# Hybrid decoder block: value products stored unfolded, division on the loaded outputs, key duplicates by DMA, twelve early gate tiles

## The chip, the core and the metric
The kernel runs on one core of a Trainium2 chip. The metric is device time in microseconds (us), the median of the runs. The engines are TensorE (PE: matmuls and transposes, with its weight loads shown as PEld), VectorE (DVE), ScalarE (ACT), GpSimd (POOL) and SyncE (SP). Each runs its own instructions in a fixed order and waits on semaphores for the others; SP and ScalarE also issue the DMAs.

## What is computed
One layer of a decoder block on x of 1024 positions by 1024 features, in float32. Four causal mixers read the same normalised input; each output is projected, gated and summed.

```python
h = rms_norm(x, norm_attn_pre)
(a_q, a_kv, a_g, b_qkv, c_qkv, c_f, d_qlat, d_kvlat, d_krope) = split_cols(h @ w_in, IN_SPLITS)
o_a = nsa_mixer(...)         # 4 heads: compressed, selected and window branch, gated
o_b = dilated_mixer(...)     # 2 heads x 3 dilations, merged by their denominators
o_c = forgetting_mixer(...)  # 4 heads, log-forget bias on the logits
o_d = mla_mixer(...)         # 4 heads, low-rank keys and values
for i, (o_i, w_i) in enumerate(branches):     # A, B, C, D
    term = sigmoid(h @ w_merge_gate[i]) * (o_i @ w_i)
    merged = term if i == 0 else merged + term
x = x + rms_norm(merged @ w_o, norm_attn_post)
```

Each attention is a softmax over the causal keys, `p / den` times the values, with a head of 64 features. A gated MLP of width 2816 with a causal convolution follows; the change does not touch it.

## The kernel before
Every float32 operand of a large product is split into two parts, `hi` (rounded) and `lo` (the remainder), and `gemm` (lines 136 to 144) runs three matmuls for each 128 rows of depth: hi by hi (L142), hi by lo (L143), lo by hi (L144). A split costs one copy on ScalarE (L119 for weights, L316 and L336 for projections) and one subtraction on VectorE or GpSimd (L120, L320).

The attention stage (to about 735 us) first makes the normalised input `H`, then runs the mixers in the order D (141 to 262), A (262 to 476), C (476 to 604) and B (604 to 731). `project` writes 512 columns of a projection into the PSUM tile `pd`; `k_pair`, `q_pair` and `v_pair` make operands of it. `k_pair` keeps two heads, each twice, on both halves of the 128 partitions, since the hi and lo queries lie in opposite halves: four ScalarE copies of 64 partitions for each 512 columns, two or four remainders on VectorE, and in the unshared form one GpSimd copy for each head.

For one head, groups of 256 queries are worked off: `softmax_rows` makes the logits `ps` of a block of 128 queries, VectorE adds the bias and takes the maximum (L382), ScalarE the exponential with the row sum `den` (L387); `normalize` takes the reciprocal (L394) and multiplies the block (L396, or L398 with a gate). `pv` then transposes the probabilities (`ptp`, L419), splits them into `th` (ScalarE) and `tl` (VectorE), and multiplies by the values (L434 to L437) into `pvt`. The upper and lower 64 partitions of `pvt` hold the hi and the lo part of the values' product, so `fold` (L443, L444) copies one half on VectorE and adds the other, into the output tile `ot`. A pair of heads fills 128 partitions of `ot`, which ScalarE's queue stores to `o_d` in HBM.

The gates are products of `H` with 128 output features m, for a branch br. `FILL` names seven (br, m) that are computed early: `fill_tile` loads two weight chunks through a single buffer `fraw`, splits them into `fh` (ScalarE) and `fl` (GpSimd), runs two halves of 24 matmuls into the single PSUM buffer `pf` at a priority far below all else, and ScalarE applies tanh (`ft`, L206) and stores to `gate_d`. The program is ordered ahead of time by a scheduler that goes by priorities and its own estimates; on the chip each engine's order is fixed.

In the stage after that (`p2`, 740 to 1089) seven output tiles are loaded (`oraw`, two buffers, L930, by ScalarE's queue) and split into `oh` and `ol`. For m = 0 to 7 then come, in the branch order D, A, C, B (3, 0, 2, 1), the gate's product `pgb` (48 matmuls, none if it is early) and the branch's product (12, and 6 for B), and VectorE and GpSimd sum into `merged`. The out-projection and the MLP follow. [rows n] further on names a group of rows of the trace, which stand in their own section below.

Of the kernel before, what the change touches and what calls it, by code (L numbers as in the profile page):

```python
# [15 lines left out]
F32 = mybir.dt.float32  # L16
# [3 lines left out]
ALU = mybir.AluOpType  # L20
# [13 lines left out]
NFILL = 7  # L34
# [51 lines left out]
def body(tc, a, out):  # L86
# [10 lines left out]
    o_d = drp.tile([896, S], F32, name="o_d")  # L97
# [16 lines left out]
    miscc = cp.tile([128, 384], F32, name="miscc")  # L114
    ident, tri, ones = miscc[:, 0:128], miscc[:, 128:256], miscc[:, 256:384]
# [60 lines left out]
    with ExitStack() as c1:  # L176
# [152 lines left out]
        def k_pair(src, kind="n", shared=False):  # L329
            ks = [ap.tile([128, S], F32R, name="ks", tag="ks", bufs=BUFS["ks"]) for _ in range(2)]  # L330
            kl = [ap.tile([128, S], F32R, name="kl", tag="kl", bufs=BUFS["kl"]) for _ in range(2)]
            for hf, ps in project(src):
                for e in range(2):
                    pe = ps[64 * e:64 * e + 64]
                    for d in range(2):
                        A.copy(permuted(ks[e][64 * d:64 * d + 64], hf, kind), psin(pe, kind))  # L336
                    if shared:
                        for d in range(2):
                            lo_of(permuted(kl[e][64 * d:64 * d + 64], hf, kind),
                                  permuted(ks[e][64 * d:64 * d + 64], hf, kind), pe, kind)  # L340
                    else:
                        lo_of(permuted(kl[e][64 * e:64 * e + 64], hf, kind),
                              permuted(ks[e][64 * e:64 * e + 64], hf, kind), pe, kind)
            if not shared:
                for e in range(2):
                    o = 64 - 64 * e
                    G.tensor_copy(kl[e][o:o + 64], kl[e][64 * e:64 * e + 64].bitcast(F32))
            return ks, kl
# [18 lines left out]
        def softmax_rows(chunks, clamp=BIG, stat=None, two=False, into=None):  # L367
# [18 lines left out]
            den = nm[:, 6:7] if stat is None else stat[1]  # L386
# [3 lines left out]
        def normalize(P, n, den, nm, gate=None, guard=False):  # L390
# [4 lines left out]
            if gate is None:  # L395
                V.tensor_scalar(P[:, 0:n], P[:, 0:n], rc, None, op0=ALU.mult)  # L396
            else:
                V.tensor_scalar(P[:, 0:n], P[:, 0:n], rc, gate, op0=ALU.mult, op1=ALU.mult)  # L398
# [47 lines left out]
        def new_pv():  # L446
            return psv.tile([128, 256], F32, name="pvt", tag="pv")

# [127 lines left out]
        hx = ap.tile([128, 2, 64], F32, name="hx")  # L576
# [7 lines left out]
        u = ap.tile([128, 128], F32, name="u")  # L584
# [83 lines left out]
        for pr in range(2):  # L668
# [23 lines left out]
            fill()  # L692
            ot = new_ot()
            for e in range(2):
                (qh, ql), (kh, kl_) = QD[e], KD[e]
# [19 lines left out]
        ks, kl = k_pair(a["win"][1], shared=True)  # L715
        va = v_pair(a["win"][2])
        for pr in range(2):
            qs = q_pair(a["win"][3 + pr])
            ot = new_ot()
            for e in range(2):  # L720
                h = 2 * pr + e
                fill()
                bias = toeplitz(h)
                for g in range(4):
# [30 lines left out]
                    fold(ot[64 * e:64 * e + 64, 256 * g:256 * g + 256], pvt, e)  # L755
            A.dma_start(o_d[128 * pr:128 * pr + 128, :], ot)
# [3 lines left out]
        for pr in range(2):  # L760
# [3 lines left out]
            ot = new_ot()  # L764
            for e in range(2):
                h = 2 * pr + e
                fill()
                nck = ap.tile([128, S], F32, name="nck", tag="bias", bufs=BUFS["bias"])
# [5 lines left out]
                for g in range(4):  # L774
                    pvt = new_pv()
                    P2 = []
                    for qb in (2 * g, 2 * g + 1):
# [7 lines left out]
                        P, n, den, nm = softmax_rows(ch)  # L785
                        normalize(P, n, den, nm)
                        P2.append(P)
                    pv(pvt, P2, causal_blocks(vc[:, e], 2 * g + 2), True, True)
                    fold(ot[64 * e:64 * e + 64, 256 * g:256 * g + 256], pvt, e)
            A.dma_start(o_d[384 + 128 * pr:384 + 128 * pr + 128, :], ot)  # L790
# [94 lines left out]
        A.dma_start(o_d[256:384, :], ot0)  # L885
# [38 lines left out]
    with pool("p2") as p2:  # L924
        branches = ((3, 640, 2), (0, 0, 2), (2, 384, 2), (1, 256, 1))
        O = {}
        for br, f0, nk in branches:
            for k in range(nk):
                raw = p2.tile([128, S], F32, name="oraw", tag="oraw", bufs=2)
                A.dma_start(raw, o_d[f0 + 128 * k:f0 + 128 * k + 128, :])  # L930
# [4 lines left out]
        for m in range(KT):  # L935
# [5 lines left out]
            pgb = {}  # L941
            te = []
            for i in [i for i, f in enumerate(FILL) if f[1] == m]:
                for hf in range(2):
                    te.append(p2.tile([128, 512], F32, name="te", tag="te", bufs=2))
                    SP.dma_start(te[hf], gate_d[i][:, 512 * hf:512 * hf + 512])

            def gate(br):
# [3 lines left out]
                for hf in range(2):  # L952
                    pgb[br, hf] = pq("pgb", "qr"[hf])
                    if not early:
                        gemm(pgb[br, hf][:, 0:512], lambda k: (gh[:, k], gl[:, k]), h_half(hf), range(KT))

            def branch(br, f0, nk):
                early = (br, m) in FILL
                kt0 = f0 // 128
                for hf in range(2):  # L960
                    c = slice(512 * hf, 512 * hf + 512)
                    t = te[hf] if early else p2.tile([128, 512], F32, name="tg", tag="tg", bufs=2)
# [365 lines left out]
```

## Time and profile before

| | us |
|---|---|
| median of 3 runs | 1878.5 |
| lowest and highest | 1878.36, 1881.29 |
| the profiled execution, its own time | 1880.98 |
| its span in the trace | 1879.2 |
| mixers D to B (window) | 590 (141 to 731) |
| gate and branch stage (window) | about 350 (740 to 1089) |

The profile is one execution; its instructions are recorded with start and length, and idle time is put down to the engine whose signal ended it. The mean granted clock of TensorE over the span was 0.991 of full speed. A matmul's record overlaps the next one's, so busy time of PE is longer than the distance between matmuls.

### The profile page before, as it was taken

Reading aid. Unit: us, or ns where it says so; the run is one execution under the profiler, and the core shown is the slowest. Engines: PE = TensorE matmul, PEld = TensorE weight load, DVE = VectorE, ACT = ScalarE, POOL = GpSimd, SP = SyncE. Lnnn points to the kernel's source line nnn. Section 1 sums busy time; section 2 is a strip of 40 time slices with the busy share of each in tenths; the row PEclk is TensorE's granted clock in tenths of the full one; section 3 lists DMA queues with packets and bytes.
Section 4 is the critical chain, followed back from the end, with each engine's and each line's share of the span. In section 5 each row is a group of like instructions: output and inputs, shape, how many; then the busy total and the mean of one; then the engine's idle time right before and its main releaser. Section 6 shows DMA issues by size and latency. Waiting matters only on the chain.

```text
span 1879.2 us, 24134 instructions
## 1 busy us (share of the span) xinstructions
PE 1817.5 (97%) x8894; PEld 1489.8 (79%) x8894; DVE 1092.4 (58%) x2110; ACT 789.7 (42%) x1467; POOL 527.6 (28%) x520
## 2 busy tenths in 40 slices
PE   7889999999999899999999999899999999999998
PEld 6767777877777787888888878688888888888786
DVE  4438869989877344322222265688676767733544
ACT  5435646656565453312112144444443434332432
POOL 3401121221122210111222201597767675100000
PEclk9999999999999999999999999899999999999999
DMA  7151110100111112311222142122222222444643
GB/s 240 49 139 41 53 58 25 36 23 24 35 44 55 31 46 85 111 63 56 76 66 61 40 179 90 59 101 90 79 76 82 79 90 68 148 144 151 224 153 111
DMA packets 55366, 158.83 MB, mean 85 GB/s; under 512 B 9344, under 2 KB 10704, under 8 KB 55248
## 3 DMA queue, kind: packets, MB, share of 16 engines
q1 hardware_dynamic: 42352, 124.09, 20.6%
q10 hardware_dynamic: 12896, 33.21, 5.0%
q8 instruction: 70, 1.15, 0.3%
q14 instruction: 48, 0.39, 0.1%
HBM read 129.91 MB, written 31.61 MB: 86 GB/s over the span
## 4 chain that ended last, share of the span: by engine, by line
PE 68%; DVE 3%; DMA 1%; ACT 1%; issue 1%; POOL 0%; SPq 0%; DVEq 0%; ACTq 0%; POOLq 0%
PE pgb L142 6%; PE pgb L143 6%; PE pgb L144 6%; PE pk L1219 4%; PE pk L1221 4%; PE pk L1220 4%; PE py L143 2%; PE py L142 2%; PE pz L143 2%; PE pz L142 2%; PE py L144 2%; PE pz L144 2%; PE px L143 2%; PE px L142 2%; PE px L144 2%; PE pd L142 2%
## 5 line engine op out<-in xcount | busy, mean ns | idle before, releaser
L142 PE MATMUL pgb<-hh,whi 128*128 128x512 f32 x400 | 155.8, 390 | 1.1 <-ACT ft L206 0.7
L144 PE MATMUL pgb<-hh,wlo 128*128 128x512 f32 x400 | 155.6, 389 | 0.0
L143 PE MATMUL pgb<-hl,whi 128*128 128x512 f32 x400 | 155.6, 389 | 0.0
L120 DVE TENSOR_TENSOR wlo<-wraw,whi 128x1024 fp32r<-128x1024 f32 x25 | 30.6, 1225 | 210.4 <-ACT whi L119 210.4
L119 ACT CAST whi<-wraw 128x1024 fp32r<-128x1024 f32 x38 | 40.0, 1053 | 233.4 <-PE pgb L143 196.3
L387 ACT ACTIVATE P<-P,nm 128x512 f32<-128x512 f32 (+7 forms) x160 | 108.1, 677 | 64.6 <-DVE nm L382 63.4
L1086 POOL TENSOR_TENSOR aset<-sums,aset 128x512 fp32r<-128x512 f32 x66 | 131.2, 1988 | 5.3 <-ACT aset L1085 5.2
L142 PE MATMUL pd<-hh,whi 128*128 128x512 f32 x320 | 129.9, 406 | 2.1 <-DVE kl L320 2.0
L425 ACT CAST th<-ptp 128x512 fp32r<-128x512 f32 (+3 forms) x202 | 96.7, 517 | 77.8 <-PE ptp L419 65.5
L144 PE MATMUL pd<-hh,wlo 128*128 128x512 f32 x320 | 129.0, 403 | 0.0
L143 PE MATMUL pd<-hl,whi 128*128 128x512 f32 x320 | 129.0, 403 | 0.0
L426 DVE TENSOR_TENSOR tl<-ptp,th 128x512 fp32r<-128x512 f32 (+3 forms) x202 | 115.3, 599 | 17.5 <-ACT th L425 15.3
L1219 PE MATMUL pk<-aset 128*128 128x512 f32 x320 | 124.6, 390 | 0.6 <-DVE y L1259 0.6
L1220 PE MATMUL pk<-aset 128*128 128x512 f32 x320 | 124.5, 390 | 0.5 <-DVE aset L120 0.5
L1221 PE MATMUL pk<-aset 128*128 128x512 f32 x320 | 124.3, 390 | 0.0
L974 POOL TENSOR_TENSOR mg<-mg,tg 128x512 f32<-128x512 f32 x32 | 42.1, 1319 | 286.1 <-DVE tg L972 241.7
L419 PE MATMUL ptp<-miscc,P 128*128 128x128 f32 x678 | 112.2, 274 | 5.9 <-DVE P L396 3.1
L423 POOL MEMSET th<- 128x128 f32 x86 | 18.9, 220 | 291.2 <-PE pvt L434 130.7
L1085 ACT CAST aset<-wraw 128x512 fp32r<-128x512 f32 x88 | 54.1, 618 | 97.7 <-PE pz L144 37.8
L419 PEld LDWEIGHTS ptp<-miscc,P 128*128 128x128 f32 x678 | 80.4, 140 | 15.5 <-DVE P L396 4.9
L120 DVE TENSOR_TENSOR aset<-at,aset 128x512 fp32r<-128x512 f32 x44 | 30.4, 692 | 106.9 <-ACT aset L119 106.8
L1085 ACT CAST aset<-sums 128x512 fp32r<-128x512 f32 x66 | 40.9, 622 | 119.5 <-PE py L144 37.1
(362 smaller groups left out, 5109.5 us busy)
## 6 DMA issues: line engine op xcount, KB each, us to landing
wraw<-in_wup SPq DMA_DIRECT2D x44, 512.0 KB, 3.6
wraw<-in_wdn SPq DMA_DIRECT2D x44, 512.0 KB, 3.5
wraw<-in_wg SPq DMA_DIRECT2D x25, 512.0 KB, 3.5
act_d<-o ACTq DMA_DIRECT2D x22, 512.0 KB, 3.9
at<-act_d SPq DMA_DIRECT2D x44, 256.0 KB, 2.6
wraw<-in_win SPq DMA_DIRECT2D x20, 512.0 KB, 3.2
x<-in_x SPq DMA_DIRECT2D x8, 512.0 KB, 6.9
wraw<-in_wo SPq DMA_DIRECT2D x8, 512.0 KB, 3.5
```

What stands on the lines that cost most here:

```text
L142: T.matmul(ps, lh, rh, start=first and ii == 0, stop=False)
L143: T.matmul(ps, lh, rl, start=False, stop=False)
L144: T.matmul(ps, ll, rh, start=False, stop=last and ii == n - 1)
L387: A.activation(P[:, 0:c0], P[:, 0:c0], AF.Exp, bias=prev, scale=-1.0, accum_out=den)
L419: T.transpose(tp[0:kr, at[x]], P2[x[1]][:, c:c + kr], ident)
L425: A.copy(th[0:kr, i0:i1], tp[0:kr, i0:i1])
L426: V.tensor_tensor(tl[0:kr, i0:i1], tp[0:kr, i0:i1], th[0:kr, i0:i1].bitcast(F32), op=ALU.subtract)
L1085: A.copy(t[:, 0], src)
L1086: eng.tensor_tensor(t[:, 1], src, t[:, 0].bitcast(F32), op=ALU.subtract)
L1219: T.matmul(ps[b][:, w], ah[:, c], wh[:, w], start=st, stop=False)
L1220: T.matmul(ps[b][:, w], ah[:, c], wl[:, w], start=False, stop=False)
L1221: T.matmul(ps[b][:, w], al[:, c], wh[:, w], start=False, stop=sp)
```

## The change
- The output tiles of A, C and D hold one head each, unfolded: ScalarE copies the whole 128x256 `pvt` into `ot`, and `keep` stores the two halves of 64 partitions into two planes of `o_d`. B still folds.
- C and D do not normalise their probabilities. Their row sums go into `dens`, whose reciprocal is taken once after C.
- In `p2` each output of A, C and D is loaded as two tiles (both through `oraw`) and added on VectorE. For C and D, ScalarE spreads the reciprocals over a tile, PE transposes it in eight blocks (`rcp`), and VectorE multiplies.
- `k_pair` makes one copy and one remainder of all 128 partitions, and six DMAs on SP's queue make the duplicates.
- `NFILL` goes from 7 to 12: the tiles (1,0), (2,7), (2,6), (2,5) and (2,4) are early as well. D calls `fill` once for each head.
- Early gate tiles are loaded from `gate_d` where the gate would be computed, into `tg` with four buffers. `hx` and `u` share buffers with `th` and `tl`.

```diff
-NFILL = 7
+NFILL = 12
...
-    o_d = drp.tile([896, S], F32, name="o_d")
+    o_d = drp.tile([2, 896, S], F32, name="o_d")
...
+    dens = cp.tile([128, 8, 8], F32, name="dens")
...
             for hf, ps in project(src):
-                for e in range(2):
-                    pe = ps[64 * e:64 * e + 64]
-                    for d in range(2):
-                        A.copy(permuted(ks[e][64 * d:64 * d + 64], hf, kind), psin(pe, kind))
...
+                hi, lo = permuted(ks[0], hf, kind), permuted(kl[0], hf, kind)
+                A.copy(hi, psin(ps, kind))
+                lo_of(lo, hi, ps, kind)
+            for t in (ks, kl):
+                for d in range(2):
+                    SP.dma_start(t[1][64 * d:64 * d + 64].bitcast(F32), t[0][64:128].bitcast(F32))
+                SP.dma_start(t[0][64:128].bitcast(F32), t[0][0:64].bitcast(F32))
...
+        def keep(row, ot):
+            for d in range(2):
+                A.dma_start(o_d[d, row:row + 64, :], ot[64 * d:64 * d + 64])
...
-                        P, n, den, nm = softmax_rows(causal_chunks(mk, qb, 0, 128 * qb + 128, causal))
-                        normalize(P, n, den, nm)
-                        P2.append(P)
+                        P2.append(softmax_rows(causal_chunks(mk, qb, 0, 128 * qb + 128, causal),
+                                               den=dens[:, qb, 4 + 2 * pr + e:5 + 2 * pr + e])[0])
                     pv(pvt, P2, causal_blocks(vd[pr][:, e], 2 * g + 2), True, True)
-                    fold(ot[64 * e:64 * e + 64, 256 * g:256 * g + 256], pvt, e)
-            A.dma_start(o_d[640 + 128 * pr:640 + 128 * pr + 128, :], ot)
+                    A.copy(ot[:, 256 * g:256 * g + 256], pvt)
+                keep(640 + 128 * pr + 64 * e, ot)
...
+        V.reciprocal(dens, dens)
...
                 raw = p2.tile([128, S], F32, name="oraw", tag="oraw", bufs=2)
-                A.dma_start(raw, o_d[f0 + 128 * k:f0 + 128 * k + 128, :])
+                A.dma_start(raw, o_d[0, r, :])
+                if br != 1:
+                    raw2 = p2.tile([128, S], F32, name="oraw", tag="oraw", bufs=2)
+                    A.dma_start(raw2, o_d[1, r, :])
+                    V.tensor_tensor(raw, raw, raw2, op=ALU.add)
+                if br > 1:
+                    h = 4 * (br - 2) + 2 * k
+                    tp = pq("rcp", "qr"[k])
+                    A.copy(raw2.rearrange("p (b h d) -> p b h d", b=8, h=2),
+                           dens[:, :, h:h + 2].unsqueeze(3).to_broadcast([128, 8, 2, 64]))
+                    for b in range(8):
+                        T.transpose(tp[:, 128 * b:128 * b + 128], raw2[:, 128 * b:128 * b + 128], ident)
+                    V.tensor_tensor(raw, raw, tp, op=ALU.mult)
```

TensorE's order at the end of the gate tiles, where the first gate products follow: `pf` are matmuls of `fill_tile`, `pgb` those of the gates of `p2`, `hh` and `hl` the two parts of the input. Before:

```order
L142 MATMUL pf<-hh_116,fh 128x512
L143 MATMUL pf<-hl_117,fh 128x512
L144 MATMUL pf<-hh_116,fl 128x512
L142 MATMUL pgb<-hh_114,whi 128x512
L143 MATMUL pgb<-hl_115,whi 128x512
L144 MATMUL pgb<-hh_114,wlo 128x512
```

The same place after; `rcp` are the transposes of the spread reciprocals, eight for each output tile of C or D:

```order
L145 MATMUL pf<-hh_122,fh 128x512
L146 MATMUL pf<-hl_123,fh 128x512
L147 MATMUL pf<-hh_122,fl 128x512
L941 MATMUL rcp<-miscc,oraw 128x128 x24
L145 MATMUL pgb<-hh_120,whi 128x512
L146 MATMUL pgb<-hl_121,whi 128x512
L147 MATMUL pgb<-hh_120,wlo 128x512
```

The transposes of three output tiles now stand between the last gate tile and the first gate product; the fourth tile's stand 40 `pgb` matmuls further on. Of the `pf` matmuls 305 of 336 stood ahead of the last transposes of mixer B (`wtp`) before, and 239 of 576 now; the other 337 stand behind them in one piece.

ScalarE's order around the first loads of the outputs: `ft` are the tanh steps of the gate tiles and `gate_d` their stores, `oraw` the loads of outputs. Before:

```order
L206 ACTIVATE ft<-pf 128x512
L885 DMA o_d<-ot 128x1024
L207 DMA gate_d_99<-ft 128x512
L206 ACTIVATE ft<-pf 128x512
L207 DMA gate_d_99<-ft 128x512
L930 DMA oraw<-o_d 128x1024 x2
L119 CAST bh<-braw 128x896
L119 CAST oh_8118<-oraw 128x1024
L119 CAST oh_8124<-oraw 128x1024
L930 DMA oraw<-o_d 128x1024 x2
```

The same place after:

```order
L209 ACTIVATE ft<-pf 128x512
L210 DMA gate_d_104<-ft 128x512
L209 ACTIVATE ft<-pf 128x512
L210 DMA gate_d_104<-ft 128x512
L929 DMA oraw<-o_d 128x1024
L932 DMA oraw<-o_d 128x1024
L122 CAST bh<-braw 128x896
L938 COPY oraw<-dens 128x1024
L929 DMA oraw<-o_d 128x1024
L122 CAST oh_8253<-oraw 128x1024
L932 DMA oraw<-o_d 128x1024
```

The first load stands behind the last gate tile's store in both, but in the changed kernel that is the twelfth tile's, each output takes two loads, and the copy of the reciprocals and the split of one output stand between the loads of the next.

## Rows read from the trace of the kernel before
**Rows 1.** The page's first part: busy us, share of the span, instructions.
```profile
PE 1817.5 (97%) x8894; PEld 1489.8 (79%) x8894; DVE 1092.4 (58%) x2110; ACT 789.7 (42%) x1467; POOL 527.6 (28%) x520
```
**Rows 2.** Windows: us, busy PE, PEld, DVE, ACT, POOL; clock, DMA share, GB/s.
```profile
141.00:731.00 590.00, 570.39 (x3348) 463.47 (x3347) 452.99 (x1320) 336.22 (x749) 116.60 (x213) 1.00 0.12 39
846.00:940.00 94.00, 94.00 (x416) 77.83 (x416) 24.31 (x28) 18.71 (x24) 18.05 (x12) 1.00 0.20 66
```
**Rows 3.** Windows, instructions of pf alone (first) and of pgb alone (two).
```profile
733.30:739.00 5.70, 5.68 (x24) 4.42 (x24) 0.00 (x0) 1.00 0.35 138
...
739.86:793.70 53.84, 53.47 (x234) 43.95 (x235) 3.94 (x6) 3.78 (x7) 1.00 0.39 130
793.70:835.86 42.16, 42.16 (x187) 34.91 (x186) 5.27 (x8) 4.37 (x8) 1.00 0.19 51
```
**Rows 4.** Chain of waits in mixer B: start us, us, engine, tile, line.
```profile
686.32 0.95 PE ps L378 x8
...
690.49 0.87 PE ptp L419 x8
```
**Rows 5.** Groups of PE, 141 to 731: busy us, mean ns; idle before, releaser.
```profile
L142 PE MATMUL pd<-hh,whi 128*128 128x512 f32 x304 | 123.7, 407 | 2.1 <-DVE kl L320 2.0
...
L142 PE MATMUL pd<-wq,qnhi 128*128 128x384 f32 x2 | 0.7, 339 | 0.0
```
**Rows 6.** Groups of DVE, line L396: 141 to 262 (D), 476 to 604 (C).
```profile
L396 DVE TENSOR_SCALAR P<-P,nm 128x128 f32<-128x128 f32 (+7 forms) x32 | 18.7, 589 | 0.2
...
L396 DVE TENSOR_SCALAR P<-P,nm 128x128 f32<-128x128 f32 (+7 forms) x32 | 18.6, 580 | 0.3
```
**Rows 7.** Groups of DVE by shape, 141 to 731.
```profile
L443 DVE COPY fo<-pvt 64x256 f32<-64x256 f32 x64 | 27.0, 422 | 15.1 <-PE pvt L437 12.4
L444 DVE TENSOR_TENSOR ot<-pvt,fo 64x256 f32<-64x256 f32 x64 | 26.9, 421 | 1.7
L394 DVE RECIPROCAL nm<-nm 128x1 f32<-128x1 f32 x160 | 24.0, 157 | 5.1 <-ACT P L387 3.8
L320 DVE TENSOR_TENSOR kl<-pd,ks 64x512 fp32r<-64x512 f32 x28 | 20.8, 742 | 19.8 <-ACT ks L336 19.5
```
**Rows 8.** Groups of ACT by shape, 141 to 731.
```profile
L336 ACT CAST ks<-pd 64x512 fp32r<-64x512 f32 x48 | 31.9, 664 | 9.9 <-DVE kl L320 5.2 <-PE pd L144 4.2
...
L425 ACT CAST th<-ptp 128x256 fp32r<-128x256 f32 x16 | 5.9, 371 | 4.9 <-PE ptp L419 4.7
```
**Rows 9.** Tile oraw: duration ns min/median/max, first and last start; DMA landing us.
```profile
L930 ACTq DMA_DIRECT2D oraw<-o_d x7: 326/326/457, 741.9 to 763.6; - x7
L119 ACT CAST oh<-oraw x7: 1046/1052/1055, 748.8 to 767.1; 128x1024 fp32r<-128x1024 f32 x7
L120 DVE TENSOR_TENSOR ol<-oraw,oh x7: 1218/1225/1227, 750.0 to 768.2; 128x1024 fp32r<-128x1024 f32 x7
...
DMA to landing us min/median/max: 4.4/4.4/4.4
```
**Rows 10.** Tile fraw, the same view: a gate tile's weight chunk and its split.
```profile
L119 ACT CAST fh<-fraw x14: 606/622/634, 38.4 to 724.6; 128x512 fp32r<-128x512 f32 x14
L120 POOL TENSOR_TENSOR fl<-fraw,fh x14: 1263/1292/1410, 39.1 to 725.3; 128x512 fp32r<-128x512 f32 x14
...
DMA to landing us min/median/max: 2.5/2.7/5.6
```
**Rows 11.** Timeline, 722 to 752: start us, us, instruction, [idle before, releaser].
```profile
730.39 0.60 PE L877 MATMUL wtp<-miscc,wx 128*128 128x128 f32 x4
...
733.32 0.50 PE L142 MATMUL pf<-hh,fh 128*128 128x512 f32 x1 [0.69 <-ACT ft L206]
...
738.78 0.39 PE L144 MATMUL pf<-hh,fl 128*128 128x512 f32 x1
...
739.86 0.50 PE L142 MATMUL pgb<-hh,whi 128*128 128x512 f32 x1 [0.69 <-ACT ft L206]
```
**Rows 12.** Window in the MLP, the columns of rows 2.
```profile
1214.00:1219.00 5.00, 5.00 (x16) 4.20 (x15) 2.72 (x5) 2.38 (x5) 3.33 (x6) 0.51 0.09 21
```

More of the change, by code (lines that the diff above doesn't have):

```diff
@@ L332, in k_pair @@
             for hf, ps in project(src):
-                for e in range(2):
-                    pe = ps[64 * e:64 * e + 64]
-                    for d in range(2):
-                        A.copy(permuted(ks[e][64 * d:64 * d + 64], hf, kind), psin(pe, kind))
[L337 to L347, printed above, removed]
+                hi, lo = permuted(ks[0], hf, kind), permuted(kl[0], hf, kind)
[5 more added lines that the diff above has]
+                SP.dma_start(t[0][64:128].bitcast(F32), t[0][0:64].bitcast(F32))
             return ks, kl
@@ L364, in v_pair, with softmax_rows @@
             return vs
-        def softmax_rows(chunks, clamp=BIG, stat=None, two=False, into=None):
+        def softmax_rows(chunks, clamp=BIG, stat=None, two=False, into=None, den=None):
             P = ap.tile([128, S], F32, name="P", tag="P", bufs=BUFS["P"]) if into is None else into
@@ L385, in softmax_rows, with normalize @@
                 c0 += n
-            den = nm[:, 6:7] if stat is None else stat[1]
+            if den is None:
+                den = nm[:, 6:7] if stat is None else stat[1]
             A.activation(P[:, 0:c0], P[:, 0:c0], AF.Exp, bias=prev, scale=-1.0, accum_out=den)
             return P, c0, den, nm
-        def normalize(P, n, den, nm, gate=None, guard=False):
+        def normalize(P, n, den, nm, gate, guard=False):
             rc = nm[:, 7:8]
@@ L394, in normalize @@
             V.reciprocal(rc, den)
[L395 to L398, printed above, removed]
+            V.tensor_scalar(P[:, 0:n], P[:, 0:n], rc, gate, op0=ALU.mult, op1=ALU.mult)
         def pv(pvt, P2, blocks, first, last):
@@ L574, in body @@
         V.tensor_tensor(cum.rearrange("p b h -> p (b h)"), pt1[:, 0:32], tot.rearrange("p b h -> p (b h)"), op=ALU.add)
-        hx = ap.tile([128, 2, 64], F32, name="hx")
+        hx = ap.tile([128, 2, 64], F32, name="hx", tag="th", bufs=BUFS["th"])
         ps = bank((128, 128))
@@ L582, in body @@
         hx = hx.rearrange("p d c -> p (d c)")
-        u = ap.tile([128, 128], F32, name="u")
+        u = ap.tile([128, 128], F32, name="u", tag="tl", bufs=BUFS["tl"])
         V.tensor_tensor(u, hx, hx, op=ALU.mult)
@@ L691, in body @@
                 QD.append(qd)
[L692 to L693 removed]
             for e in range(2):
+                fill()
+                ot = new_ot()
                 (qh, ql), (kh, kl_) = QD[e], KD[e]
@@ L754, in body @@
                     pv(pvt, P2, [((0, 0), 128, VC)] + bl, False, True)
-                    fold(ot[64 * e:64 * e + 64, 256 * g:256 * g + 256], pvt, e)
-            A.dma_start(o_d[128 * pr:128 * pr + 128, :], ot)
+                    A.copy(ot[:, 256 * g:256 * g + 256], pvt)
+                keep(128 * pr + 64 * e, ot)
         for pr in range(2):
@@ L784, in body @@
                             ch.append((ps_, n, nck[:, kk:kk + n]))
-                        P, n, den, nm = softmax_rows(ch)
-                        normalize(P, n, den, nm)
-                        P2.append(P)
+                        P2.append(softmax_rows(ch, den=dens[:, qb, h:h + 1])[0])
                     pv(pvt, P2, causal_blocks(vc[:, e], 2 * g + 2), True, True)
-                    fold(ot[64 * e:64 * e + 64, 256 * g:256 * g + 256], pvt, e)
-            A.dma_start(o_d[384 + 128 * pr:384 + 128 * pr + 128, :], ot)
+                    A.copy(ot[:, 256 * g:256 * g + 256], pvt)
+                keep(384 + 128 * pr + 64 * e, ot)
+        V.reciprocal(dens, dens)
         st0 = ap.tile([128, 8, 2, 2], F32, name="st0")
@@ L940, in body @@
             split_weights(bh, bl, braw, V, 1.0)
[L941 to L946, printed above, removed]
+            pgb, tg = {}, {}
             def gate(br):
@@ L952, in gate @@
                 for hf in range(2):
+                    tg[br, hf] = p2.tile([128, 512], F32, name="tg", tag="tg", bufs=4)
+                    if early:
+                        SP.dma_start(tg[br, hf], gate_d[FILL.index((br, m))][:, 512 * hf:512 * hf + 512])
                     pgb[br, hf] = pq("pgb", "qr"[hf])
@@ L961, in branch @@
                     c = slice(512 * hf, 512 * hf + 512)
-                    t = te[hf] if early else p2.tile([128, 512], F32, name="tg", tag="tg", bufs=2)
+                    t = tg[br, hf]
                     pg, pb = pgb[br, hf][:, 0:512], pgb[br, hf][:, 512:1024]
```

11 lines of the change are left out of this document (6 added, 5 removed).

## The prediction
> **What bounds the kernel now.** The page's busy shares come first: TensorE (PE) is busy 97% of the span and VectorE (DVE) 58% [rows 1]. An average hides where PE waits, so the table of windows comes next. In the gate and branch stage PE is busy 94.00 of 94.00 us; in the attention stage, 141 to 731, 570.39 of 590.00 [rows 2]. That busy time is no floor: a matmul's record is longer than its distance from the next one. In the gate stage 186 matmuls of 512 columns take 42.16 us [rows 3], 0.2267 each. The chain of waits has eight of 256 columns in 0.95 us and eight transposes in 0.87 [rows 4], so 0.119 and 0.109 each. The grouped view of PE for 141 to 731 has 36 groups, of which the first and the last stand in [rows 5]; summed by size, they are 1270 of 512 columns, some 1020 of 256 or fewer, 132 of 384 (taken between, 0.175) and 814 transposes. The sum is 288 + 121 + 23 + 89, with a few us for unrecorded ones about 526. So PE waits some 64 of the 590 us. That is what less work on VectorE and ScalarE (ACT) could give back. Nothing else in the diff touches PE's own count of columns except 56 added transposes.
>
> **What leaves the attention stage.** On VectorE: the multiplications by the reciprocal in D and C, 18.7 and 18.6 us [rows 6]; 64 of the reciprocals at 0.157, 10.0; 48 of the 64 folds at 0.422 + 0.421, 40.5; and the key remainders, 28 of 64 partitions for 20.8 us, become 12 of full height at the same 0.74, 8.9, so 11.9 saved [rows 7]. Together 99.7 of 453 busy us. On ScalarE 48 key copies of 31.9 us become 12 at 0.664, 8.0, and 48 evacuations of 128x256 come in, at 0.371 by the nearest row, 17.8 [rows 8]; with 18 more store issues at 0.33 [rows 9] its load stays as it was.
> How much of PE's 64 us of waiting goes? A softmax block runs VectorE, ScalarE, VectorE, PE, ScalarE, VectorE, PE in turn; the relief takes out the second VectorE step in C and D and half a step at each group's end, while mixer B keeps its folds, and A its normalization. I take half, **-32**, with 0 and -64 as bounds: no row shows the freed steps alone.
> The key duplicates are six copies of 256 KB in two steps. A gate chunk of the same size lands in 2.7 us (5.6 at most) [rows 10], so the keys come about 5.4 us later; the 48 matmuls of the query projection that follow (10.9 us) cover that. I take 0; uncovered parts of it and SP's own order may cost up to 6.
>
> **Where the five added gate tiles go.** This is read from the order of instructions. Before, some 305 of the 336 gate matmuls of `fill_tile` stand ahead of the last transposes `wtp` of mixer B and 30 behind. After, 239 of 576 stand ahead and 337 behind, with nothing else between them: fourteen halves of 24 and one more. So the change does not put five more tiles into PE's gaps; it takes 66 matmuls out, 66 x 0.227 = **-15**, and makes a solid tail.
> A half tile in such a tail costs 6.54 us: its first matmul starts at 733.32 and the first of the next group at 739.86. 24 matmuls are 5.70 us of window [rows 3] and the rest is the wait for the tanh that empties the only `pf` buffer (0.69 idle by the row at 739.86 [rows 11]). Fourteen are 91.6, less 1.1 for the wait after the last. To that comes feeding: the second chunk's load can start only when the first chunk's remainder has freed `fraw`, and then 2.7 us of DMA, 0.62 of cast and 1.29 of remainder follow [rows 10]. Against the matmul that wants them I find 0.2 to 0.8 us late in each of six tiles; I add 3. Behind `wtp` there were 7.8 us of tail before (731.0 to 738.8, the start of the last gate matmul [rows 11]). So 91.6 - 1.1 + 3 - 7.8 = **+85.7**, with -3 to +8 around it.
>
> **The start of the gate stage.** Call E the start of the last `pf` matmul. Before, E is 738.8, the next matmuls of `pgb` follow at once, and the loads of the mixers' outputs (`oraw`, 741.9 to 763.6) run beside them [rows 9, 11]; m = 1 begins at 793.70 [rows 3], E + 54.9. After, PE's order has the 24 transposes `rcp` of three output tiles ahead of its first `pgb`, and ScalarE's has the first `oraw` load behind the last `ft` store of the last gate tile. So nothing of the loads is hidden under the tail, and PE stands still until three tiles have been worked through, two `oraw` buffers for two loads each.
> By durations: first issue E + 3.1 as before, second 0.33 later, landing after 4.4: E + 7.8. A tile of D or C is then 4.4 load, 1.22 addition, 1.05 copy of the divisors, 0.87 transposes, 1.22 multiplication (the two full-width rows, 1.046 to 1.055 and 1.218 to 1.227, are the nearest to these new steps), 1.05 and 1.22 for the split [rows 4, 9], and six hand-overs of about 0.1: 11.6. A tile of A lacks the copy, the transposes and the multiplication: 8.05. Two of D, two of A, and 3.3 to the transposes of the first C tile: 7.8 + 23.2 + 16.1 + 3.3 = E + 50.4. Then 40 `pgb` matmuls (9.1, and 2.5 more for the clock, below), the second C tile's `rcp` at E + 62.0, 56 + 24 matmuls (18.1), gate 2's 48 (10.9) and 18 of products (4.1): E + 95.6 with half a us of hand-overs, against 54.9: **+40.7**. The new order alone decides this: before, the same stretch of PE work hid the loads.
> Bounds: the loads between 2.7 and 5.6 us, the ends of [rows 10], move six serial waits by -10 to +7. The clock: in the 5 us from 1214, after PE had waited for VectorE twice, the granted clock was 0.51, which is 1.2 GHz of 2.4, and 16 matmuls and transposes took all 5 us [rows 12]; 2.5 is taken, 0 to 5 is the bound.
> By the Trainium skill's page "DMA: Bandwidth & Descriptors", section "Anatomy of one DMA — SWDGE (gpsimd) path", a transfer is about 2.0 us plus its bytes at 436 GB/s. For half a megabyte that is an estimate of 3.2 us, 1.2 under the 4.4 that this trace shows; over six serial loads it would make the time some 7 us shorter, about 1907. The page fits that line to the path of GpSimd, these loads are issued by ScalarE, and the trace decides.
>
> **Later in the stage.** For m = 4 to 7 another gate is ready early: 4 x 48 x 0.2267 = **-43.5** (m = 0's is in the sum above). The remaining 31.3 us for each m still exceed VectorE's and ScalarE's share there (24.31 and 18.71 of 94 [rows 2]), and the tiles come back through four buffers, loaded ahead on SP, so I see no new wait.
>
> **Sum.** 1880.98 is the profiled execution's own time. 1880.98 - 32 - 15 + 85.7 + 40.7 - 43.5 = 1916.9. It lies 2.5 above the median of the three runs, 1878.5, so the forecast is **1914 us**, slower by 1.9%.
>
> **The rivals.**
> First, faster: mixers A, C and D become bound by PE alone. My floor rests on 0.109 for a transpose; a 512-column matmul's rate would make it 0.227 / 4 = 0.057, and 814 of them 42 us less, so that up to 64 + 42 = 106 us could go from attention, instead of 32. From 32 + 36 = 68 us the kernel is no slower than before, from 72 faster by 0.2%; with 85 of them gone it is 1861. For it: VectorE, which stands in every block's chain, loses a fifth of its work here (99.7 of 453). Against it: ScalarE is not relieved, PE's gaps were already filled with 66 more gate matmuls, and 68 is more than all the waiting that the rows' rates leave. 6% for faster, 3% for within 0.2%.
> Second, the relief gives nothing: PE keeps its waits because the exponentials, the evacuations on ScalarE and the duplicates set them. Then 1914 + 32 = 1946. 18%.
> Third, the early tiles do what early tiles are for: all 14 halves lie in gaps and the loads stay hidden. Then 1880.98 - 32 - 54.4 (five tiles of 48) - 7.8 - 2.5 = 1784. The order speaks against every part of it; 1%.
> Fourth, the loads are quicker and overlap more than I let them: 1914 - 10 to 15, about 1901; that lies in the forecast's own range.
>
> **How the numbers follow.** The forecast (half of the waits, tail and serial loads as worked out) has 72%, and holds 1890 to 1938. The range reaches down for most of the recovered waits (1914 - 32 = 1882) and up for none recovered (1946): **1882 to 1948**, which leaves the faster rival and a sum of late loads outside, about 2 in 10. A measurement of this kernel can tell about 0.2% from no change (1874.7 to 1882.3): faster 6%, same 4%, slower 90%.
>
> **What would show it.** The window between the last `wtp` and the last `pf` should be near 93 us, filled by `pf` at 6.5 us a half. Then PE should be idle for nearly all of some 50 us, with only 24 `rcp` in them and a low clock behind. The `oraw` loads should begin after the last store to `gate_d`. The end of `wtp`, 731 before, should come near 684; 716 would mean that the relief gave nothing, 648 or less that the first rival holds. Each m from 4 on should take 31 us. If `oraw` loads are seen under the tail, or `rcp` is waited for under 30 us, the term of +40.7 is wrong; if half tiles take 5.7 us instead of 6.5, the tail is 11 us shorter.

## The result and the profile after

The changed kernel takes 1937.89 us (median of 4 runs, 1936.98 to 1940.18) against 1878.5 before: a ratio of 1.0314, with a 95% interval of 1.0296 to 1.0332. The profiled execution took 1938.66, its span is 1936.9. That is 59 us slower, where 36 had been forecast; the time lies inside the range (1882 to 1948), near its upper end.

The page's first and fourth part and its line of the granted clock, of the changed kernel (the first answers to [rows 1]):

```profile
PE 1827.2 (94%) x8926; PEld 1499.9 (77%) x8926; DVE 1024.1 (53%) x1876; ACT 782.0 (40%) x1488; POOL 522.7 (27%) x520
...
PEclk9999999999999999779999999989999999999999
...
PE 85%; DVE 5%; ACT 4%; DMA 3%; issue 1%; POOL 1%; SPq 0%; ACTq 0%; DVEq 0%; POOLq 0%
```

TensorE (PE) gained only 10 us of busy time, VectorE (DVE) lost 68. The clock shows a hole in two of the forty slices, about 775 to 872 us, that the kernel before did not have: PE stood still there. To see where the 57.7 us of span come from, both traces are cut at the same five moments (starts of the last `wtp`, of the last `pf`, of the gates of m = 1, of the first out-projection matmul `pk`):

| stretch | before | after | difference | forecast |
|---|---|---|---|---|
| start of the span to the last `wtp` | 730.7 | 703.3 | -27.5 | -47 |
| last `wtp` to last `pf` (tail of gate tiles) | 8.1 | 91.9 | +83.8 | +85.7 |
| last `pf` to m = 1 (start of the gate stage) | 54.9 | 96.2 | +41.3 | +40.7 |
| m = 1 to the first `pk` | 295.1 | 255.9 | -39.2 | -43.5 |
| first `pk` to the end of the span | 790.4 | 789.6 | -0.8 | 0 |

Windows of the changed kernel: attention, the tail, the standing start, and the work up to m = 1 (columns as in [rows 2]):

```profile
152.00:703.50 551.50, 539.31 (x3231) 446.41 (x3229) 356.11 (x1055) 315.83 (x750) 99.28 (x199) 1.00 0.22 60
...
703.50:795.50 92.00, 82.31 (x338) 61.91 (x336) 3.00 (x4) 16.18 (x27) 17.06 (x13) 1.00 0.24 80
795.50:846.50 51.00, 5.54 (x25) 4.70 (x25) 14.47 (x12) 8.84 (x9) 0.00 (x0) 0.53 0.39 126
846.50:891.40 44.90, 44.90 (x197) 37.09 (x196) 14.81 (x15) 10.98 (x14) 3.65 (x3) 0.96 0.20 61
```

The second row is the tail: 338 matmuls, nothing else of weight on any engine. The third is the standing start: 51 us with 5.54 of PE work, at a mean granted clock of 0.53 (close to 1.2 GHz of 2.4). None of the compute engines is busy for even a third of it.

PE's timeline in these two stretches (start us, us, instruction, [idle before, releaser]; the rows answer to [rows 11]):

```profile
702.93 0.60 PE L875 MATMUL wtp<-miscc,wx 128*128 128x128 f32 x4
...
704.53 0.50 PE L145 MATMUL pf<-hh,fh 128*128 128x512 f32 x1 [0.77 <-ACT ft L209]
...
783.13 0.50 PE L145 MATMUL pf<-hh,fh 128*128 128x512 f32 x1 [0.69 <-ACT ft L209]
...
789.68 0.50 PE L145 MATMUL pf<-hh,fh 128*128 128x512 f32 x1 [0.69 <-ACT ft L209]
...
807.43 1.97 PE L941 MATMUL rcp<-miscc,oraw 128*128 128x128 f32 x8 [11.89 <-ACT oraw L938]
...
818.92 1.97 PE L941 MATMUL rcp<-miscc,oraw 128*128 128x128 f32 x8 [9.52 <-ACT oraw L938]
...
844.93 1.97 PE L941 MATMUL rcp<-miscc,oraw 128*128 128x128 f32 x8 [24.05 <-ACT oraw L938]
```

Half tiles follow each other at 6.55 us (783.13 to 789.68). Behind the last one PE waits 11.89, 9.52 and 24.05 us for three output tiles (the two tiles of A, which need no `rcp`, are worked through in the last of these waits), and only then gets its first gate matmul. The chain of waits tells what an output tile costs (start us, us, what):

```profile
796.21 2.00 DMA gate_d<-ft
798.28 0.33 ACTq L929
798.64 5.44 DMA oraw<-o_d
804.09 0.23 DVE bl L123
804.32 0.76 issue
805.08 1.23 DVE oraw L933
806.33 1.05 ACT oraw L938
807.43 1.98 PE rcp L941 x8
809.44 1.23 DVE oraw L942
810.69 1.05 ACT oh L122
811.77 1.24 DVE ol L123
813.03 3.51 DMA oraw<-o_d
...
844.93 1.97 PE rcp L941 x8
846.90 0.43 PE pgb L145
847.33 0.43 PE pgb L146
```

From one load's wait to the next, 807.43 to 818.92, a tile of D takes 11.5 us: load, addition, copy, transposes, multiplication, split, one after the other. The first gate matmuls behind the stand are 0.43 us apart, at half the speed of [rows 3].

### The profile page after: what moved, and what is told of

The parts are those of the page before. It is cut to its first block, busy times and chain, and to the rows that moved or that the text cites. A ratio compares the mean times of both kernels' runs of the same rounds, so it can differ in the third digit from the quotient of the medians.

```text
span 1936.9 us, 24144 instructions
## 1 busy us (share of the span) xinstructions
PE 1827.2 (94%) x8926; PEld 1499.9 (77%) x8926; DVE 1024.1 (53%) x1876; ACT 782.0 (40%) x1488; POOL 522.7 (27%) x520
## 4 chain that ended last, share of the span: by engine, by line
PE 85%; DVE 5%; ACT 4%; DMA 3%; issue 1%; POOL 1%; SPq 0%; ACTq 0%; DVEq 0%; POOLq 0%
PE pgb L145 5%; PE pgb L146 5%; PE pgb L147 4%; PE ps L377 4%; PE pd L145 4%; PE pd L147 4%; PE pd L146 4%; PE pk L1228 4%; PE pk L1230 4%; PE pk L1229 4%; PE ptp L414 4%; PE pvt L429 2%; PE pf L145 2%; PE pvt L430 2%; PE py L146 2%; PE py L145 2%
## 5 line engine op out<-in xcount | busy, mean ns | idle before, releaser
L983 POOL TENSOR_TENSOR mg<-mg,tg 128x512 f32<-128x512 f32 x44 | 59.8, 1370 | 301.9 <-DVE tg L981 301.2
L145 PE MATMUL pgb<-hh,whi 128*128 128x512 f32 x320 | 125.8, 393 | 2.1 <-DVE tg L981 2.1
L1095 POOL TENSOR_TENSOR aset<-sums,aset 128x512 fp32r<-128x512 f32 x66 | 125.1, 1895 | 4.7 <-ACT aset L1094 4.5
L420 ACT CAST th<-ptp 128x512 fp32r<-128x512 f32 (+3 forms) x202 | 97.0, 518 | 70.8 <-PE ptp L414 57.7
L146 PE MATMUL pgb<-hl,whi 128*128 128x512 f32 x320 | 125.2, 391 | 0.0
L147 PE MATMUL pgb<-hh,wlo 128*128 128x512 f32 x320 | 125.0, 391 | 0.0
L122 ACT CAST whi<-wraw 128x1024 fp32r<-128x1024 f32 x33 | 34.7, 1052 | 186.3 <-PE pgb L146 161.4
L123 DVE TENSOR_TENSOR wlo<-wraw,whi 128x1024 fp32r<-128x1024 f32 x20 | 24.5, 1225 | 155.2 <-ACT whi L122 155.2
L414 PEld LDWEIGHTS ptp<-miscc,P 128*128 128x128 f32 x678 | 81.6, 140 | 11.6 <-DVE P L393 4.0
L145 PE MATMUL pf<-hh,fh 128*128 128x512 f32 x192 | 78.8, 411 | 11.8 <-ACT ft L209 11.8
```

The lines of the kernel that those rows point to most:

```text
L145: T.matmul(ps, lh, rh, start=first and ii == 0, stop=False)
L146: T.matmul(ps, lh, rl, start=False, stop=False)
L147: T.matmul(ps, ll, rh, start=False, stop=last and ii == n - 1)
L414: T.transpose(tp[0:kr, at[x]], P2[x[1]][:, c:c + kr], ident)
L420: A.copy(th[0:kr, i0:i1], tp[0:kr, i0:i1])
L1095: eng.tensor_tensor(t[:, 1], src, t[:, 0].bitcast(F32), op=ALU.subtract)
```

## The experiments

The theory after the result: the tail and the standing start cost what the order of instructions says, and the relief of attention is smaller than forecast. Rivals: the five added gate tiles are the whole loss; the serial loads, and not the place of `rcp`, hold the gate stage back; and for attention, either PE had little to give back, or the gate tiles had already used what there was.

Most of these kernels ran once, with the kernel before beside them on the same chip. On one chip 15 runs of the kernel before lie between 1875.52 and 1881.36 us, so a difference of 1 to 3 us between single runs shows nothing.

**Seven tiles in the changed kernel.**

```diff
-NFILL = 12
+NFILL = 7
```

> The changed kernel with seven early gate tiles instead of twelve. In its order 239 gate matmuls stand ahead of wtp, as in the changed kernel, and 97 behind (337 there). My theory (the loss is a tail of half tiles at 6.54 us each and a gate stage that stands still at its start): wtp ends at about 703 as before; tail about 26 us instead of 92; then 107 us from the last pf to m = 1 (96 plus the gate that is no longer early); then the kernel before's 42.2 us for each m. Span about 1921, so 16 under the changed kernel and 42 over the kernel before. Rival (the five tiles are the whole loss): a span within 5 us of 1879.

Span 1920.5, time 1922.34 (the kernel before on the same chip 1878.68). The last `wtp` starts at 703.71, and the four halves behind it follow at 6.55 us:

```profile
704.94 0.50 PE L145 MATMUL pf<-hh,fh 128*128 128x512 f32 x1 [0.73 <-ACT ft L209]
711.49 0.50 PE L145 MATMUL pf<-hh,fh 128*128 128x512 f32 x1 [0.69 <-ACT ft L209]
...
741.97 1.97 PE L941 MATMUL rcp<-miscc,oraw 128*128 128x128 f32 x8 [11.51 <-ACT oraw L938]
```

That is PE's timeline of this kernel. The last `pf` is at 730.1 and m = 1 begins at 836.2, 106.1 later. By time, 43.7 us are lost without the five tiles (1922.34 against 1878.68), and the tiles are the other 15.6 (1937.89 against 1922.34).

**Twelve tiles in the kernel before.**

```diff
-NFILL = 7
+NFILL = 12
...
-                    te.append(p2.tile([128, 512], F32, name="te", tag="te", bufs=2))
...
+                    tg[br, hf] = p2.tile([128, 512], F32, name="tg", tag="tg", bufs=4)
+                    if early:
+                        SP.dma_start(tg[br, hf], gate_d[FILL.index((br, m))][:, 512 * hf:512 * hf + 512])
```

> The kernel before with twelve early gate tiles, loaded back as in the change, and nothing else changed. Its order has 305 gate matmuls ahead of wtp and 271 behind, and no rcp. My theory: wtp at 731, a tail of about 74 us instead of 8, the gate stage at once behind it with the loads hidden, five gates less there (-54 and about 4 back at the ends): span about 1895, 16 over the kernel before. With the run of seven tiles in the changed kernel (+42) this adds up to the change's +58. Rival (early tiles are free, and the loss is the unfolding and division alone): 1880 or less.

Span 1892.3, time 1894.3 (1878.68 before): +15.6 where +16 was expected, so that with the 43.7 of the first run the two parts add up to the whole. The last `pf` is at 804.3, m = 1's gates at 848.0, 43.7 later. A gate matmul costs 0.2267 us in the gate stage, and 6.55 / 24 = 0.273 in a tail, where each half waits for the tanh that empties `pf`. An early tile is worth something only in a gap.

**No early tiles, in both kernels.** In each, one edit:

```diff
+NFILL = 0
```

> The kernel before without early gate tiles: its attention stage shows its own waits, with nothing to fill them. The last wtp ended at 730.7 with 305 gate matmuls (69 us) ahead of it. Theory one (PE's visible idle time of 18 us between 152 and 731 is all that was to be had; the rest is spacing of matmuls): without them wtp ends near 731 - 69 + 10 = 672. Theory two (the gate matmuls hid most of the waits): near 700. To be set against the next run.

> The changed kernel without early gate tiles. Theory one: the relief of VectorE is worth what it was with the tiles in place, some 12 us of waits: wtp ends about 12 us before that of the kernel before without tiles. Theory two (the waits were hidden by gate matmuls, so relief and tiles took the same time twice): 25 to 40 us before it. In both the start of the gate stage stands still for some 45 us and more, with rcp ahead of the first gate.

The last `wtp` starts at 721.6 in the first and at 694.8 in the second. Both expectations for the first run were too early: attention without tiles ends only 9.1 us sooner than with 305 gate matmuls in it, which are 69 us of PE's work. So the tiles ran nearly free. Windows of the mixers, from the first transposes `krp` of D to the last `wtp` (columns as in [rows 2]): the kernel before, the same without tiles, the changed kernel, the same without tiles.

```profile
148.40:730.70 582.30, 564.22 (x3318) 458.42 (x3319) 446.54 (x1298) 334.72 (x746) 115.31 (x212) 1.00 0.12 38
...
138.30:721.60 583.30, 544.03 (x3109) 435.87 (x3110) 446.84 (x1298) 325.20 (x730) 104.41 (x204) 0.97 0.09 31
...
148.20:703.20 555.00, 542.79 (x3252) 449.47 (x3253) 359.37 (x1059) 317.90 (x752) 99.28 (x199) 1.00 0.22 60
...
139.70:694.80 555.10, 524.88 (x3109) 430.57 (x3110) 360.25 (x1059) 312.65 (x742) 91.91 (x194) 0.98 0.21 55
```

The matmul counts show what fills the waits: 209 of the tiles' matmuls in the kernel before, 143 in the changed one. In neither do they make the mixers longer (582.3 against 583.3, 555.0 against 555.1); the 9 us that the tiles cost lie ahead of D, where 96 of their matmuls stand and `krp` comes 10 us later with them. PE's recorded idle time is 39.3 us without tiles and 18.1 with them in the kernel before, 30.2 and 12.2 in the changed one.

The relief shortens the mixers by 28.2 us without tiles and by 27.3 with them. That is in the range of theory two, but with the tiles in place the relief takes off as much, which neither theory had said. Its price comes later. With the waits shorter, the order puts 66 fewer tile matmuls among the mixers; they had been free there, and behind the last `wtp` each costs 0.273 us. In the run of seven tiles the last `wtp` comes 27.0 us earlier than in the kernel before and the tail is 18.3 longer, so that the last `pf`, when all seven tiles are done, comes 8.7 earlier (730.1 against 738.8). In this sense relief and tiles drew on the same waits.

**The changed kernel without the division.**

```diff
-                if br > 1:
-                    h = 4 * (br - 2) + 2 * k
-                    tp = pq("rcp", "qr"[k])
...
-                    V.tensor_tensor(raw, raw, tp, op=ALU.mult)
```

> The changed kernel without the division of C's and D's outputs (left out: the spread copy, the 32 transposes rcp and the multiplications, so outputs of C and D stay undivided); the two-plane loads and additions stay. Its order has 96 gate matmuls right behind the last pf. Theory (the standing start comes from rcp ahead of the gates, and the serial loads are then partly hidden): from the last pf to m = 1 some 65 us instead of 96, span about 1907. Rival (the serial loads through two buffers alone hold the stage back): the same 96 us, about 1935.

Span 1897.7, 39 us under the changed kernel and 9 under the theory; from the last `pf` to m = 1 are 61.7 us (65 expected, 96.2 with the division). PE's timeline from the last `pf` on, all its waits up to 860:

```profile
794.87 0.50 PE L145 MATMUL pgb<-hh,whi 128*128 128x512 f32 x1 [0.69 <-ACT ft L209]
822.03 0.73 PE L145 MATMUL pgb<-oh,bh 128*128 128x512 f32 x2 [2.35 <-ACT oh L122]
830.30 0.73 PE L145 MATMUL pgb<-oh,bh 128*128 128x512 f32 x2 [0.27 <-ACT oh L122]
838.65 0.73 PE L145 MATMUL pgb<-oh,bh 128*128 128x512 f32 x2 [1.94 <-ACT oh L122]
840.02 0.50 PE L146 MATMUL pgb<-ol,bh 128*128 128x512 f32 x1 [0.64 <-DVE ol L123]
848.07 1.22 PE L145 MATMUL pgb<-oh,bh 128*128 128x512 f32 x2 [6.86 <-ACT oh L122]
853.02 0.73 PE L145 MATMUL pgb<-oh,bh 128*128 128x512 f32 x2 [1.62 <-ACT oh L122]
```

The loads still come one pair after the other, but behind 96 gate matmuls, and the waits add up to some 14 us instead of 45. What it leaves out is work of PE, VectorE and ScalarE as well; the run of unfolded stores further down, which normalises the blocks instead, takes that objection away. Neither run keeps the division in this stage with `rcp` behind the gates. So what the place of `rcp` costs, and what the longer chain of each divided tile (copy, transposes and multiplication, 4.2 us by the chain rows above) adds, was not taken apart.

**Old key duplicates, and the new ones alone.** The first is the run of seven tiles with `k_pair` as before, the second the kernel before with the new `k_pair` only.

```diff
-                for e in range(2):
-                    pe = ps[64 * e:64 * e + 64]
-                    for d in range(2):
-                        A.copy(permuted(ks[e][64 * d:64 * d + 64], hf, kind), psin(pe, kind))
...
+                A.copy(hi, psin(ps, kind))
+                lo_of(lo, hi, ps, kind)
...
+                    SP.dma_start(t[1][64 * d:64 * d + 64].bitcast(F32), t[0][64:128].bitcast(F32))
```

> The changed kernel with seven early gate tiles and with the key duplicates of the kernel before (copies on ScalarE, remainders on VectorE, copies on GpSimd). Its order has 279 gate matmuls ahead of wtp and 57 behind, where the run of seven tiles has 239 and 97. If the duplicates by DMA freed no wait of PE: wtp 9 us later than 703.7, tail 10 us shorter, the sum as in the run of seven tiles (1922). If they freed waits of about 4 us: 1926. If the DMAs cost time: under 1920.

> The kernel before with the key duplicates by DMA and nothing else. 57 gate matmuls behind wtp instead of 31. Attention ends 6 us earlier for the 26 that moved and some 3 for waits freed, wtp at 722; the tail is 2.4 halves of 6.54, 15.5 instead of 8. Sum -2, 1877: not to be told from no change. If the copies on ScalarE and VectorE had held PE up much more: 1870.

The first: 1927.56 (span 1925.8), 5 us over the run of seven tiles; last `wtp` 720.7, last `pf` 736.1. The second: 1874.39 against 1878.16, ratio 0.9979 (0.9970 to 0.9989); last `wtp` 718.6, last `pf` 734.0, 4.8 us sooner than before. The duplicates by DMA cost nothing that shows and free about 4 us (3.8 by the medians), where 1 to 2 had been expected.

**The division alone.** The kernel before; C and D are not normalised in the blocks, and `divide` runs once for each pair of heads on the folded `ot`, inside attention.

```diff
+        def divide(ot, h):
+            V.reciprocal(dens[:, :, h:h + 2], dens[:, :, h:h + 2])
...
+                for b in range(4):
+                    T.transpose(tp[:, b], rb[:, 512 * hb + 128 * b:512 * hb + 128 * b + 128], ident)
+                V.tensor_tensor(ot[:, cs(hb)], ot[:, cs(hb)], tp.rearrange("p b k -> p (b k)"), op=ALU.mult)
...
-                        normalize(P, n, den, nm)
```

> The kernel before with only the division of C and D taken out of the blocks and done once for each pair of heads on the folded output inside attention; old folds, old keys, seven tiles. The order has 79 gate matmuls behind wtp. All 336 are done at the start of the last pf, so that moment compares the kernels: 738.8 before, 734.0 with the key DMAs alone, 730.1 in the run of seven tiles with all three parts, 736.1 in it without the key DMAs. If the multiplications L396 were what PE waited for in C and D: 731 to 733. If PE was covered by gate matmuls there: 737, no gain beyond the noise.

1879.3 (1879.72 before on that chip). Last `wtp` 718.8, last `pf` 739.9, 1.1 later than before, though 47 us of multiplications and reciprocals have left VectorE. `wtp` came 12 us earlier, but 48 more gate matmuls now stand behind it, and in the tail they cost 48 x 0.273 = 13.1 us. The run also brings 32 transposes `rcp` into attention, 3.5 us of PE's work at the 0.109 of [rows 4]. Net nothing is gained.

**Unfolded stores and key DMAs, without the division.** The run of seven tiles with `normalize` in C and D as before and no `rcp`.

> The changed kernel with seven early tiles, C and D normalised block by block as before, so that unfolded stores and key DMAs are left and no rcp. 93 gate matmuls behind wtp. Last pf at 730 to 731 if the unfolding and the keys are all of the gain in attention, at 734 if the unfolding gives nothing. From the last pf to the first out-projection matmul 375 to 380 us, against 350.0 before and 401.2 in the run of seven tiles with rcp: two thirds or more of what that stage lost comes from rcp's place in PE's order, the rest from thirteen loads through two buffers.

1879.42 (1879.72 before). The last `pf` is at 732.8, and the first `pk` at 1089.8: 357.0 us between, where the kernel before has 350.0 and the run of seven tiles 401.2. My expectation gave the thirteen loads a third of the loss (375 to 380); they cost 7 of the 51, and the division in that stage 44. In attention, the last `pf` at 732.8 lies between the two expectations: 1.2 us sooner than with the key DMAs alone (734.0), 2.7 later than with the division as well (730.1). Between single runs that is no more than a hint that unfolding and division each give a little. PE's timeline of the whole first part of the gate stage, 733 to 792, has two waits:

```profile
733.86 0.50 PE L144 MATMUL pgb<-hh,whi 128*128 128x512 f32 x1 [0.69 <-ACT ft L208]
761.90 0.80 PE L144 MATMUL pgb<-oh,bh 128*128 128x512 f32 x2 [3.27 <-ACT oh L121]
```

**Division in place, five tiles.** The kernel before with `divide` as above, the key DMAs, and the copy in `fold` on ScalarE (`hx` and `u` share buffers as in the change, here and in the run of the division alone); the gate stage is left as it was.

```diff
-NFILL = 7
+NFILL = 5
...
-            V.tensor_copy(tmp[o_], pvt[s_])
+            A.copy(tmp[o_], pvt[s_])
```

> The kernel before with the reliefs that need nothing in the gate stage: key duplicates by DMA; the copy of fold on ScalarE instead of VectorE; C and D not normalised, their folded outputs divided once for each pair of heads inside attention (transposed reciprocals, two multiplications of 128x512); five early tiles. 224 gate matmuls ahead of wtp, 16 behind. By PE's work: -18.4 for 81 matmuls fewer ahead of wtp, -10 for waits freed, so wtp at 702; tail 4.4 instead of 8; gate stage at once behind, two gates more there, +21.8. Sum -10, 1868. If the waits freed are none: 1878.

1871.03 against 1878.16, ratio 0.9962 (0.9948 to 0.9976): faster than the kernel before by 0.4%: -7.1 us where -10 was expected. The key DMAs alone gave 3.8; what the other parts and the two tiles fewer give was not taken apart. Its windows of attention and of the start of the gate stage:

```profile
152.00:701.70 549.70, 540.42 (x3236) 444.68 (x3234) 369.81 (x1095) 327.36 (x765) 98.24 (x198) 1.00 0.19 54
706.00:760.00 54.00, 52.67 (x231) 43.28 (x232) 16.80 (x17) 15.32 (x19) 5.12 (x4) 1.00 0.40 136
```

The last `wtp` starts at 701.7 (702 expected), the last `pf` at 705.3, and PE is idle for 9.3 us of attention, for 18.1 before. The last row shows the stage that stood still in the changed kernel: 52.67 busy of 54.

## Why the prediction was right, and where its size failed

**The tail** was right: +83.8 for +85.7. A half costs 6.55, as the last half before had shown in [rows 11]. The 3 us for feeding did not come: the wait ahead of nearly every half is the same 0.69 for the tanh.

**The standing start** was right in its place and its sum, +41.3 for +40.7, with errors that cancel, which is luck. The loads were quicker, 3.4 to 3.8 us in the chain, for 4.4 [rows 9]. The first piece of 5.44 need not be a load alone: VectorE's next instruction there was the split `bl` of the branch's weights, and the first addition started behind it, at 805.08. The tile view of `oraw` in the changed kernel:

```profile
L929 ACTq DMA_DIRECT2D oraw<-o_d x7: 326/327/327, 798.3 to 858.5; - x7
...
DMA to landing us min/median/max: 3.5/3.7/3.8
```

The 4.4 was of loads that ran in pairs beside others. The Trainium skill's page "DMA: Bandwidth & Descriptors", section "Anatomy of one DMA — SWDGE (gpsimd) path", gives by a fit to that path an estimate of 3.2 for the size; this run's 3.7 lies 0.5 over that and 0.7 under the 4.4, so that for loads that come alone the page was nearer. Against that the eight transposes took 1.97 us where [rows 4] had 0.87: PE had been idle ahead of each such group of eight, and its granted clock was 0.53 over the stand. A tile of D came to 11.5 us for 11.6, the third `rcp` to 844.9, 49.8 after the last `pf`, for 50.4. The sentence that the new order alone decides this term was tested only by leaving the division out of the stage: with the thirteen loads but no division it loses 7 us, with it 51. How much of that is the order and how much the longer chain stays open.

**The gates taken out** gave 39.2 for 43.5. From m = 4 to the first `pk` are 129.4 us, 32.3 for each m instead of 31.3. Part of that is new waits, in the groups of PE from 890 to 1148:

```profile
L145 PE MATMUL pgb<-hh,whi 128*128 128x512 f32 x272 | 106.2, 390 | 2.1 <-DVE tg L981 2.1
...
L145 PE MATMUL pk<-woh,mh 128*128 128x512 f32 x1 | 0.5, 506 | 0.8 <-DVE tg L981 0.8
```

With one gate fewer, PE now waits for VectorE to empty a PSUM buffer, which "I see no new wait" had excluded: 2.9 of the 4.2 us. For the rest no wait is recorded.

**Attention is where the sum failed in size**: -47 forecast, -27.5 measured, which is 19.5 of the 24 us between the forecast and the result. The -47 was added up from "I take half, **-32**" for the relief and "66 x 0.227 = **-15**" for the gate matmuls taken out. The term that failed most is the -15. It gives each of the 66 matmuls its full length, but they stood in waits: all 209 of the tiles' matmuls among the mixers cost nothing there (582.3 us with them, 583.3 without). What they cost behind the last `wtp` the forecast had counted already, in the tail. No run takes just those 66 out of the kernel before, so the 0 in place of the 15 is read from the two pairs of runs with and without tiles. The relief itself is worth 28.2 us without tiles and 27.3 with them, 4 to 5 under the 32. That half of 64 came so near is luck, as no row had shown the freed steps, and "with 0 and -64 as bounds" said so.

The 64 itself was the distance of 590 us to a floor built from the tightest rows. PE's recorded idle time, about 20 of 590 [rows 2], is no price of relief either: without tiles the relief lowers it by 9 us where the mixers get 28.2 shorter. The other 19 come out of busy time, 544.03 to 524.88 for the same 3109 matmuls. A record of some 0.39 us is longer than the 0.227 between two starts, so that a short wait need not show as idle; and the mean granted clock rose from 0.97 to 0.98. How the 19 divide between the two was not measured.

Of the parts of the relief, the key duplicates alone show a gain clear of noise (ratio 0.9979), with 12 us taken off VectorE, 24 off ScalarE and 10.6 off GpSimd (its ten copies of `kl`). The division, 47 of the 100 us taken off VectorE, gave nothing net by itself. Why the keys count for more was not tried. What PE's idle time is put down to in attention, before (141 to 731) and after (141 to 703.5):

```profile
L419 PE MATMUL ptp<-miscc,P 128*128 128x128 f32 x678 | 112.2, 274 | 5.9 <-DVE P L396 3.1 <-DVE P L398 2.7
L435 PE MATMUL pvt<-tl,vs 128*64 128x256 f32 x286 | 69.7, 289 | 3.6 <-POOL tl L424 2.8 <-DVE tl L426 0.6
...
L414 PE MATMUL ptp<-miscc,P 128*128 128x128 f32 x678 | 110.5, 273 | 4.9 <-DVE P L393 4.8
L430 PE MATMUL pvt<-tl,vs 128*64 128x256 f32 x286 | 70.2, 290 | 1.3 <-POOL tl L419 1.3
L430 PE MATMUL pvt<-tl,vd 128*64 128x256 f32 x80 | 19.8, 297 | 2.5 <-POOL tl L419 2.5
```

The 3.1 us for the multiplications of D and C (L396) are gone, but the gated multiplication of A (L398 before, L393 after), which the change does not touch, now ends 4.8 us of idle time, the largest share of 13.9, where it ended 2.7. The zeros that GpSimd writes into `tl` (L424 before, L419 after) end 3.8 for 2.8. A wait that is taken away at one step is in part taken over by the next.

A slip without weight in the sum: the "56 added transposes" are 32, as the counts of the page show (8926 and 8894).

The rivals: the second named the time best (1946, for 1937.89; the forecast was 1914), but not for its reason, since the relief did shorten the mixers. The third, that the early tiles lie in gaps, fell as the order said. What would show each step had been named: the tail near 93 (91.9), the stand near 50 (51), `wtp` near 684, with 716 for no relief: it came at 703, between the two. The 716 had the -15 in it as well; without that, no relief would have been 731.

## What to carry to other kernels

Before adding up the gain from relief on a helper engine and the gain from filler that moves away (work put into waits, here the gate tiles), ask where the filler ran: filler in a wait is free, so taking it out gives nothing back. Behind the last gap it costs its full length and its own hand-overs, so count in the order of instructions how much of it is left over. Neither the distance to a floor nor recorded idle time is the price of relief; here a run of both kernels without the filler gave it. A small step on the bound engine that needs late data (24 transposes here) should not stand ahead of work that is ready; here dividing inside attention kept the gate stage running.

## What the runs showed of the hardware

The early tiles also keep PE's clock up. Without them, the mean granted clock over attention is 0.97, with them 1.00 (the window rows above and [rows 2]). In the stretches of the kernel without tiles (D, A, C and B):

```profile
152.00:268.60 116.60, 101.46 (x547) 79.26 (x546) 91.61 (x235) 60.49 (x121) 17.61 (x35) 0.94 0.08 29
268.60:476.80 208.20, 197.13 (x1173) 158.26 (x1172) 184.45 (x620) 124.80 (x319) 39.20 (x92) 0.97 0.07 25
476.80:604.00 127.20, 127.08 (x757) 100.75 (x757) 99.09 (x279) 75.09 (x166) 27.75 (x51) 1.00 0.12 44
604.00:721.60 117.60, 104.71 (x556) 86.26 (x554) 60.11 (x135) 56.08 (x109) 19.49 (x25) 0.96 0.11 32
```

It falls where PE has waits (15.1 us of 116.6 in D, 0.94), and not in C, where it has next to none (0.1 of 127.2). At the lower of its two levels a matmul of 512 columns takes 0.43 us (the chain rows behind the standing start, where the granted clock was 0.50 from 846.9 to 849.4) for 0.227 [rows 3]. So a wait can cost more than its length, through slower matmuls, and a filler in the wait can give both back; the forecast of attention had left that out.
